# The engines' queue order taken from the tile framework's time-line simulation, in a four-layer encoder kernel

## Chip, cores and metric

The kernel runs on one core of one Trainium2 chip. The metric is the device time of one execution in microseconds: three runs gave 1616.33, 1617.34 and 1620.15, median 1617.34.

## What is computed

The input x is one sequence of 256 tokens with 1024 channels in fp32. Four layers follow one another, each a mixer and an MLP on a residual stream, and a last norm:

```python
for i in range(DEPTH):                       # DEPTH = 4
    kind = i % 3                             # 0: SSD, 1: dilated attention, 2: differential attention
    h = rmsnorm(x, norm_mix_g[i])
    h = ssd_mixer(h, ...) or dilated_mixer(h, ...) or diff_mixer(h, ...)
    x = x + h
    x = x + sqrelu_mlp(rmsnorm(x, norm_mlp_g[i]), mlp_w1[i], mlp_w2[i])
return rmsnorm(x, final_norm_g)
```

So the stages are mix0 (SSD), mlp0, mix1 (dilated), mlp1, mix2 (differential), mlp2, mix3 (SSD), mlp3. The SSD mixer projects h to a gate z, to x, B and C, which pass a convolution of width 5 over time, and to a step width dt; it scans in two directions over chunks of 128 tokens, multiplies with silu(z), norms and projects back. The MLP is square(relu(h @ w1)) @ w2 with 4096 hidden channels.

## The kernel before

Activations lie in SBUF with channels on the partitions and the 256 tokens along the free dimension. All weights are streamed from HBM in chunks of 128 x 1024 fp32. Each chunk goes through three engines: SP issues its load into `raw` (L98, 5 buffers), ACT copies it to the rounded high part `whi` (L110), DVE computes the low part `wlo` = raw - whi (L112; 5 buffers each). PE then does three matmuls for each tile of 128 x 128 (L149 high x high, L150 high x low of the activation, L151 low x high), 256 columns wide. A few chunks of the SSD mixers are used in fp32 as they are (L147).

PSUM banks are named r0 to r3 and a0 to a3. The projections of a mixer alternate between r0 and r1; DVE and ACT empty a bank before its next use. In the SSD mixers a bank of x, B or C is emptied by the convolution: ACT L469, then eight steps of DVE L475 on `cvx`, `cvB` or `cvC`, ACT L477 and DVE L478. A bank of z is emptied by L460 to L463.

At the start of a mixer the norm is finished: PE sums squares over the partitions (`sums`, L274), DVE takes the reciprocal root in small steps (`rsqrt`, L260 to L265) and makes a diagonal matrix `dg` (L282), PE broadcasts it (L283), ACT copies it to `rbc` (L284); then the eight blocks of the normalised activation follow: DVE L304 (`nf`), ACT L305 (high part `nh`), DVE L306 (low part `nl`). The first projections of a mixer (in mix0 and mix3 z0 and z1) use the raw activation (`spl`) instead and are scaled afterwards, so they need no norm.

The step width of an SSD mixer is a chain of some twenty small DVE steps on `dt_t` (`dt_post`, L507 to L529, three of its exponentials on ACT L527). After L521 PE forms running sums with L536 (`dt_sums`), ACT copies them to `rows` (L548) and sends them to DRAM (L550); from there ACT's queue loads them back, broadcast over the partitions, into `bc` (L567, two buffers, 32 loads for both SSD mixers), and DVE adds a mask (L570). ACT's exponentials L595, DVE's product L608 and the scan's matmuls L620 use the result, one pair of `bc` for each of eight groups.

In mix1 the same pattern of projections is followed by scores (L130, L131, L149 to L151 on q and k), the chunks of v (L828 to L830, 384 columns), softmax and output chunks; DVE L142 writes low parts of keys. In mix2 scores, softmax and differences follow.

Two things set the order. The program hands its steps to the framework in an order written by hand: each step has a time in CFG, CFG0, DIL or DIFF, and `emit_events` sorts by it. The framework then builds each engine's queue itself: it runs a simulation of the engines, and puts down an instruction when that simulation finds it ready, the lower number of `tc.cur_priority` first. Only the conversions are shifted in that number, by `TUNE` (L110 and L112, in `_conv`). `take`, `done` and `pump` keep the conversions three to five chunks ahead of their use. An engine works its queue in this order, and an instruction that waits for a semaphore holds back those behind it.

## Time and profile before

| | |
|---|---|
| median of three runs | 1617.34 us |
| the profiled execution's own time | 1616.8 us |
| its span | 1615.0 us |
| PE busy | 1579.2 us, 98% |
| DVE busy | 1193.0 us, 74% |
| ACT busy | 959.2 us, 59% |
| HBM read | 296.41 MB, 186 GB/s over the span |

The stages lie in the span at about: mix0 0 to 257 us, mlp0 to 430, mix1 to 720, mlp1 to 892, mix2 to 1030, mlp2 to 1190, mix3 to 1440, mlp3 to 1590. The profile's page has one row of digits for each engine over 40 equal slices, the busy share in tenths; a row of windows gives busy time and number of instructions for PE, PE's weight load, DVE, ACT and POOL in one stretch, then PE's granted clock as a share of full speed, the DMA share and GB/s. A row of the time line has start, duration, engine, line, operation, output and inputs, and in brackets the idle time of the engine before it with what ended it. A row of waits has the total, how often, and the longest.

### The profile page before, as it was taken

Reading aid. Unit: us, or ns where it says so; the run is one execution under the profiler, and the core shown is the slowest. Engines: PE = TensorE matmul, PEld = TensorE weight load, DVE = VectorE, ACT = ScalarE, POOL = GpSimd, SP = SyncE. Lnnn points to the kernel's source line nnn. Section 1 sums busy time; section 2 is a strip of 40 time slices with the busy share of each in tenths; the row PEclk is TensorE's granted clock in tenths of the full one; section 3 lists DMA queues with packets and bytes.
Section 4 is the critical chain, followed back from the end, with each engine's and each line's share of the span. In section 5 each row is a group of like instructions: output and inputs, shape, how many; then the busy total and the mean of one; then the engine's idle time right before and its main releaser. Section 6 shows DMA issues by size and latency. Waiting matters only on the chain.

```text
span 1615.0 us, 32385 instructions
## 1 busy us (share of the span) xinstructions
PE 1579.2 (98%) x13018; PEld 1534.2 (95%) x13018; DVE 1193.0 (74%) x1996; ACT 959.2 (59%) x1627; POOL 133.1 (8%) x122
## 2 busy tenths in 40 slices
PE   8999999999999999999999999999999999999998
PEld 7989899999989999999999999999998898899997
DVE  6999998555776667666555899755578999985554
ACT  5577866444566666764444677644455777664444
POOL 0012131000200000010000100100010231310001
PEclk9999999999999999999999999999999999999999
DMA  6677765665565555546566575566656677656661
GB/s 210 216 217 235 218 198 177 214 212 188 150 172 166 166 158 168 161 132 200 184 186 190 157 216 151 173 197 191 191 161 183 211 219 226 214 176 190 193 194 65
DMA packets 230294, 299.84 MB, mean 186 GB/s; under 512 B 16496, under 2 KB 166256, under 8 KB 230144
## 3 DMA queue, kind: packets, MB, share of 16 engines
q1 hardware_dynamic: 209552, 262.51, 53.1%
q10 hardware_dynamic: 20592, 35.27, 7.6%
q8 instruction: 102, 1.67, 0.4%
q14 instruction: 48, 0.39, 0.1%
HBM read 296.41 MB, written 3.62 MB: 186 GB/s over the span
## 4 chain that ended last, share of the span: by engine, by line
PE 75%; DVE 13%; DMA 5%; ACT 3%; issue 2%; POOL 0%; SPq 0%; DVEq 0%; ACTq 0%; POOLq 0%
PE r L149 13%; PE r L151 13%; PE r L150 13%; PE a L149 8%; PE a L150 8%; PE a L151 8%; DVE wlo L112 3%; DMA raw<-in_ssd_in_w_dram 2%; PE r L147 2%; DMA bc<-scr 1%; PE a L829 1%; PE a L830 1%; PE a L828 1%; PE r L620 1%; ACT whi L110 1%
## 5 line engine op out<-in xcount | busy, mean ns | idle before, releaser
L112 DVE TENSOR_TENSOR wlo<-raw,whi 128x1024 fp32r<-128x1024 f32 (+1 forms) x490 | 591.3, 1214 | 301.6 <-ACT whi L110 299.9
L110 ACT CAST whi<-raw 128x1024 fp32r<-128x1024 f32 (+1 forms) x490 | 503.1, 1034 | 450.6 <-PE r L150 224.4
L151 PE MATMUL r<-spl,wlo 128*128 128x256 f32 x1248 | 352.1, 282 | 3.7 <-DVE wlo L112 3.7
L149 PE MATMUL r<-spl,whi 128*128 128x256 f32 x1248 | 353.5, 283 | 0.5 <-ACT whi L110 0.5
L150 PE MATMUL r<-spl,whi 128*128 128x256 f32 x1248 | 353.2, 283 | 0.4
L149 PE MATMUL r<-nh,whi 128*128 128x256 f32 (+1 forms) x1024 | 291.6, 285 | 6.7 <-DVE kl L142 3.2
L151 PE MATMUL r<-nh,wlo 128*128 128x256 f32 (+1 forms) x1024 | 286.9, 280 | 2.2 <-DVE wlo L112 2.2
L150 PE MATMUL r<-nl,whi 128*128 128x256 f32 (+1 forms) x1024 | 286.8, 280 | 0.0
L150 PE MATMUL a<-hl,whi 128*128 128x256 f32 x1024 | 286.0, 279 | 0.0
L149 PE MATMUL a<-hh,whi 128*128 128x256 f32 x1024 | 286.0, 279 | 0.0
L151 PE MATMUL a<-hh,wlo 128*128 128x256 f32 x1024 | 285.6, 279 | 0.0
L151 PEld LDWEIGHTS r<-spl,wlo 128*128 128x128 f32 x1248 | 238.5, 191 | 4.3 <-DVE wlo L112 4.1
L150 PEld LDWEIGHTS r<-spl,whi 128*128 128x128 f32 x1248 | 239.1, 192 | 1.3 <-DVE spl L233 1.1
L149 PEld LDWEIGHTS r<-spl,whi 128*128 128x128 f32 x1248 | 238.7, 191 | 1.1 <-ACT whi L110 0.7
L149 PEld LDWEIGHTS r<-nh,whi 128*128 128x128 f32 (+1 forms) x1024 | 193.4, 189 | 11.0 <-issue 6.1
L151 PEld LDWEIGHTS r<-nh,wlo 128*128 128x128 f32 (+1 forms) x1024 | 193.3, 189 | 3.2 <-DVE wlo L112 2.4
L150 PEld LDWEIGHTS r<-nl,whi 128*128 128x128 f32 (+1 forms) x1024 | 193.8, 189 | 0.7 <-DVE nl L306 0.2
L149 PEld LDWEIGHTS a<-hh,whi 128*128 128x128 f32 x1024 | 193.4, 189 | 0.2 <-ACT whi L110 0.2
L150 PEld LDWEIGHTS a<-hl,whi 128*128 128x128 f32 x1024 | 193.5, 189 | 0.0
L151 PEld LDWEIGHTS a<-hh,wlo 128*128 128x128 f32 x1024 | 192.4, 188 | 0.0
L246 POOL TENSOR_TENSOR sqacc<-sqacc,sq 128x256 f32<-128x256 f32 x48 | 43.3, 901 | 1100.8 <-ACT sq L244 1099.1
L595 ACT ACTIVATE e<-bc,tb 128x256 f32<-128x256 f32 (+1 forms) x256 | 95.5, 446 | 1.5 <-issue 1.5
(249 smaller groups left out, 2400.8 us busy)
## 6 DMA issues: line engine op xcount, KB each, us to landing
raw<-in_mlp_w_dram SPq DMA_DIRECT2D x256, 512.0 KB
raw<-in_ssd_in_w_dram SPq DMA_DIRECT2D x96, 512.0 KB
bc<-scr ACTq DMA_DIRECT2D x32, 768.0 KB
raw<-in_dil_qkv_w_dram SPq DMA_DIRECT2D x48, 512.0 KB
raw<-in_ssd_out_w_dram SPq DMA_DIRECT2D x32, 512.0 KB
raw<-in_dil_qkv_w_dram SPq DMA_DIRECT2D x64, 192.0 KB
raw<-in_diff_qkv_w_dram SPq DMA_DIRECT2D x24, 512.0 KB
raw<-in_dil_out_w_dram SPq DMA_DIRECT2D x8, 512.0 KB
```

Source lines behind the costliest of these rows:

```text
L110: self.nc.scalar.copy(out=hi[:, :n], in_=raw[:, :n])
L112: self.nc.vector.tensor_tensor(out=lo[:, :n], in0=raw[:, :n], in1=hi[:, :n].bitcast(F32), op=ALU.subtract)
L147: mm(out, lhsT=wh, rhs=xh, start=start, stop=stop, skip_group_check=True)
L149: mm(out, lhsT=wh, rhs=xh, start=start, stop=False, skip_group_check=True)
L150: mm(out, lhsT=wh, rhs=xl, start=False, stop=False, skip_group_check=True)
L151: mm(out, lhsT=wl, rhs=xh, start=False, stop=stop, skip_group_check=True)
L246: nc.gpsimd.tensor_tensor(out=self.sqs[0], in0=self.sqs[0], in1=sq, op=ALU.add)
L595: X = lambda o, i_, bias: nc.scalar.activation(out=o, in_=i_, func=AF.Exp, bias=bias)
L620: nc.tensor.matmul(b[(h % 2) * 64:(h % 2) * 64 + 64, n * T:(n + 1) * T], lhsT=xt[:, 1 - i, h * 64:(h + 1) * 64], rhs=G[h][:, i * T:(i + 1) ...
L828: mm(o, lhsT=nh[:, k, t], rhs=w_h, start=k == 0, stop=False)
L829: mm(o, lhsT=nh[:, k, t], rhs=w_l, start=False, stop=False)
L830: mm(o, lhsT=nl[:, k, t], rhs=w_h, start=False, stop=k == 7)
```

## The change

`TileContext` gets one more argument. The simulation by which the framework builds the queues is then the one that lays instructions on time lines, instead of the simpler one that it runs by default. The instructions, their shapes and the tiles' names are the same; the order on each engine is another, and with it the wait for each semaphore and the buffer that a tile gets.

```diff
-    with tile.TileContext(nc) as tc:
+    with tile.TileContext(nc, schedule_with_timeline_sim=True) as tc:
         program(tc, aps)
```

The order differs in the mixers and at the beginnings of the stages; the middles of the MLPs have the same order on PE, DVE and ACT before and after, and SP's queue of weight loads is nearly the same. Three places follow. The number behind a name tells tiles of the same name apart.

PE at the start of mix0, before. `r0_275` and `r1_370` are the banks of z0 and z1, `a0_220` that of the norm's sums, `whi_177` and `wlo_178` the high and low part of a chunk of z0's weight:

```order
L149 MATMUL r1_370<-spl_110,whi_206 128x256
L150 MATMUL r1_370<-spl_111,whi_206 128x256
L151 MATMUL r0_275<-spl_150,wlo_178 128x256
L149 MATMUL r0_275<-spl_150,whi_177 128x256
L274 MATMUL a0_220<-guard1024_91,sq0_184 128x1 x4
L150 MATMUL r0_275<-spl_151,whi_177 128x256
```

And after, the end of z0 and z1, with the sums behind them. `r2_337`, `r0_470` and `r1_529` are the banks of dt, x0 and C0:

```order
L150 MATMUL r1_370<-spl_166,whi_212 128x256
L151 MATMUL r1_370<-spl_165,wlo_213 128x256
L274 MATMUL a0_220<-guard1024_91,sq0_184 128x1 x4
L283 MATMUL a0_220<-dg_238,ones_87 128x256
L149 MATMUL r2_337<-nh_243,whi_200 64x256
L149 MATMUL r0_470<-nh_243,whi_302 128x256
L149 MATMUL r1_529<-nh_243,whi_364 128x256
L150 MATMUL r2_337<-nl_244,whi_200 64x256
```

The sums of squares (L274) have moved from between two matmuls of z0 to behind the last of z0 and z1, 65 rows later, and the broadcast (L283) follows them at once.

DVE in mix3, before. `dt_t_14981` is the chain of the step width, `cvx_15129` the convolution of an x unit that leaves bank r1:

```order
L520 SCALAR_TENSOR_TENSOR dt_t_14981<-dt_t_14981 128x128
L475 SCALAR_TENSOR_TENSOR cvx_15129<-r1_15087,vec_76,cvx_15129 128x255
L521 SCALAR_TENSOR_TENSOR dt_t_14981<-dt_t_14981,eal_14807 128x128
L475 SCALAR_TENSOR_TENSOR cvx_15129<-r1_15087,vec_76,cvx_15129 128x255
L524 TENSOR_SCALAR dt_t_14981<-dt_t_14981 128x128
L475 SCALAR_TENSOR_TENSOR cvx_15129<-r1_15087,vec_76,cvx_15129 128x255
L525 TENSOR_SCALAR dt_t_14981<-dt_t_14981 128x128
L475 SCALAR_TENSOR_TENSOR cvx_15129<-r1_15087,vec_76,cvx_15129 128x255
L528 TENSOR_TENSOR dt_t_14981<-dt_t_14981 128x128
L475 SCALAR_TENSOR_TENSOR cvx_15129<-r1_15087,vec_76,cvx_15129 128x254
```

And after, where the same steps of the chain stand in the convolutions of later units (`cvC_15200`, `cvx_15281`):

```order
L520 SCALAR_TENSOR_TENSOR dt_t_14981<-dt_t_14981 128x128
L475 SCALAR_TENSOR_TENSOR cvx_15281<-r1_15239,vec_76,cvx_15281 128x255 x2
L521 SCALAR_TENSOR_TENSOR dt_t_14981<-dt_t_14981,eal_14807 128x128
L475 SCALAR_TENSOR_TENSOR cvx_15281<-r1_15239,vec_76,cvx_15281 128x255
L478 SCALAR_TENSOR_TENSOR cvC_15200<-th_15199,cvC_15200 128x512
L475 SCALAR_TENSOR_TENSOR cvx_15281<-r1_15239,vec_76,cvx_15281 128x255
L524 TENSOR_SCALAR dt_t_14981<-dt_t_14981 128x128
L475 SCALAR_TENSOR_TENSOR cvx_15281<-r1_15239,vec_76,cvx_15281 128x254 x2
L525 TENSOR_SCALAR dt_t_14981<-dt_t_14981 128x128
L475 SCALAR_TENSOR_TENSOR cvx_15281<-r1_15239,vec_76,cvx_15281 128x254 x2
```

From the same conversion (`wlo_15196`) on, L521 has 41 instructions before it now: 5 of L112 (itself among them), 22 of L475, 2 of L478 and 12 steps of the chain. Up to the first L570 they are 65: 6, 33, 4 and 22. Further down the mask on the first rows that come back stands in the middle of the convolution of a B unit (`cvB_15345`):

```order
L475 SCALAR_TENSOR_TENSOR cvB_15345<-r0_15299,vec_76,cvB_15345 128x255 x3
L112 TENSOR_TENSOR wlo_15422<-raw_15278,whi_15421 128x1024
L475 SCALAR_TENSOR_TENSOR cvB_15345<-r0_15299,vec_76,cvB_15345 128x255
L475 SCALAR_TENSOR_TENSOR cvB_15345<-r0_15299,vec_76,cvB_15345 128x254
L570 TENSOR_TENSOR bc_15233<-bc_15233,cst_77 128x4x256
L112 TENSOR_TENSOR wlo_15487<-raw_15308,whi_15486 128x1024
L475 SCALAR_TENSOR_TENSOR cvB_15345<-r0_15299,vec_76,cvB_15345 128x254 x2
L570 TENSOR_TENSOR bc_15236<-bc_15236,cst_77 128x4x256
```

Before, both L570 stood around two steps of `cvx_15281`, with no conversion between them. On PE, L536 stands 34 rows later than before in mix3 (row 9262 instead of 9228) and 22 rows later in mix0 (276 instead of 254).

PE in mix1, before. `r0_5663` and `r1_5740` are the banks of two projections that follow one another:

```order
L151 MATMUL r0_5663<-nh_5183,wlo_5556 128x256
L149 MATMUL r0_5663<-nh_5183,whi_5555 128x256
L150 MATMUL r0_5663<-nl_5184,whi_5555 128x256
L151 MATMUL r0_5663<-nh_5183,wlo_5556 128x256
L149 MATMUL r1_5740<-nh_5183,whi_5590 128x256
L150 MATMUL r1_5740<-nl_5184,whi_5590 128x256
```

And after, where a second set of scores (10 matmuls of L130, L131, L149 to L151 into `r2_5809` and `r3_5810`) and matmuls of v (L828 to L830 into `a0_5842` and `a1_5843`, 17 in all) come between the two; here the last of them:

```order
L828 MATMUL a0_5842<-whi_5720,nh_5183 128x384
L829 MATMUL a0_5842<-wlo_5721,nh_5183 128x384
L830 MATMUL a0_5842<-whi_5720,nl_5184 128x384
L875 MATMUL a2_5835<-head_75,S_5649 128x128 x4
L828 MATMUL a1_5843<-whi_5720,nh_5183 128x384
L829 MATMUL a1_5843<-wlo_5721,nh_5183 128x384
L149 MATMUL r1_5740<-nh_5183,whi_5590 128x256
L150 MATMUL r1_5740<-nl_5184,whi_5590 128x256
```

The first matmul into `r1_5740` has moved behind work that doesn't use that bank. Elsewhere in the mixers the same kind of thing is seen: output chunks of mix0 and mix3 stand up to 20 us earlier on PE, counted in the times that these matmuls had before, and at the starts of mix0 and mix3 DVE has all eight L304 and both L460 ahead of the first L306.

## The prediction

> **What bounds the kernel now.** I read the page first, then the waits of PE, then windows around the longest of them, then time lines of the two places where the order changes most. From the page:
>
> ```profile
> span 1615.0 us, 32385 instructions
> ...
> PE 1579.2 (98%) x13018; PEld 1534.2 (95%) x13018; DVE 1193.0 (74%) x1996; ACT 959.2 (59%) x1627; POOL 133.1 (8%) x122
> ...
> DVE  6999998555776667666555899755578999985554
> ...
> PE 75%; DVE 13%; DMA 5%; ACT 3%; issue 2%; POOL 0%; SPq 0%; DVEq 0%; ACTq 0%; POOLq 0%
> ```
>
> PE is busy for 98% of the span, so all that a new order can take away from PE is the 35.8 us in which it stands (1615.0 - 1579.2), plus the time that it runs at a reduced clock. DVE is at 74% over the whole, but the row of slices has eight or nine tenths in the first six slices and the five around 1240 to 1440 us, which are the two SSD mixers (mix0 and mix3). There DVE has almost nothing to spare, and 13% of the chain goes through it. What PE waits for:
>
> ```profile
> PE r L151 <- DVE wlo L112: 5.8, 2, 3.7
> ...
> PE a L274 <- POOL sqacc L246: 4.5, 3, 2.4
> ...
> PE r L149 <- DVE kl L142: 3.2, 1, 3.2
> ...
> PE r L149 <- DVE cvx L475: 3.2, 4, 1.5
> ...
> PE a L151 <- DVE wlo L112: 2.5, 1, 2.5
> ...
> DVE bc L570 <- DMA bc<-scr: 7.4, 6, 2.5
> ```
>
> Columns: total, times, longest. Few long waits make up most of the 35.8 us: 3.7 for a weight's low part in mix0, 2.4 for a sum of squares at mix1's start, 3.2 for a bank that DVE empties in mix1, 2.5 in mix3's output. The last row is DVE's own: it waits for rows that come back from DRAM.
>
> Windows around the long waits (busy us and number of instructions of each engine, then PE's granted clock):
>
> ```profile
> 14.00:19.00 5.00, 0.85 (x6) 0.45 (x4) 4.79 (x9) 4.71 (x8) 0.00 (x0) 0.98 0.60 214
> ...
> 19.00:26.00 7.00, 6.95 (x33) 6.86 (x34) 5.52 (x13) 0.14 (x1) 0.00 (x0) 0.53 0.70 200
> ...
> 26.00:40.00 14.00, 13.79 (x105) 12.55 (x104) 12.54 (x26) 9.60 (x18) 0.00 (x0) 1.00 0.52 160
> ...
> 436.00:443.00 7.00, 7.00 (x36) 6.95 (x36) 2.82 (x10) 1.26 (x2) 4.41 (x13) 0.57 0.30 79
> ...
> 443.00:475.00 32.00, 31.45 (x248) 31.14 (x248) 26.67 (x48) 21.32 (x38) 0.00 (x0) 1.00 0.68 169
> ...
> 480.00:484.00 4.00, 4.00 (x25) 4.00 (x24) 2.75 (x6) 1.67 (x6) 0.00 (x0) 0.62 0.65 180
> ...
> 1200.00:1204.00 4.00, 4.00 (x23) 4.00 (x23) 2.57 (x9) 1.04 (x1) 0.00 (x0) 0.59 0.29 84
> ```
>
> After each of these waits PE's clock falls to about a half for some microseconds. From 19 to 26 us 33 matmuls take 7.0 us; at the pace of the next row (13.79 / 105 = 0.131 us) they would take 4.3, so 2.7 are lost. From 436: 36 at 31.45 / 248 = 0.127 us make 4.6, so 2.4 lost. From 480: 25 make 3.2, so 0.8 lost; from 1200: 23 make 2.9, so 1.1 lost. [...]
>
> The stages themselves, in equal stretches:
>
> ```profile
> 40.00:80.00 40.00, 39.83 (x288) 37.65 (x287) 38.39 (x83) 21.82 (x47) 2.57 (x2) 1.00 0.69 212
> ...
> 1280.00:1320.00 40.00, 39.82 (x297) 35.43 (x296) 38.93 (x60) 29.21 (x60) 11.97 (x5) 1.00 0.72 225
> ...
> 320.00:360.00 40.00, 40.00 (x342) 40.00 (x342) 22.56 (x22) 18.74 (x21) 0.00 (x0) 1.00 0.70 224
> ...
> 780.00:820.00 40.00, 40.00 (x342) 40.00 (x341) 22.76 (x23) 18.71 (x22) 0.00 (x0) 1.00 0.61 190
> ...
> 1040.00:1080.00 40.00, 40.00 (x355) 40.00 (x354) 23.34 (x23) 19.07 (x23) 0.00 (x0) 1.00 0.64 196
> ...
> 1480.00:1520.00 40.00, 40.00 (x355) 40.00 (x354) 22.46 (x23) 19.21 (x23) 0.00 (x0) 1.00 0.64 195
> ```
>
> In the SSD mixers (the first two) DVE is busy for 38.4 and 38.9 of 40 us and PE for all of it: both bound it, and any wait that falls on DVE is paid again by PE. In the four MLPs PE is full and DVE half empty. There the order of the instructions does not change, but the same matmuls ran at two paces: 342 in 40 us in two of them, 355 in the other two.
>
> **The change part by part.** Nothing is computed differently: PE's 1579 us of work stay. So the sum consists of waits that go, the clock that goes with them, and waits that come. I take the places in order of time.
>
> *Start of mix0.* DVE's low part comes ahead of its copies, so the wait of 3.7 us at 15.1 goes, and the 2.7 us of clock behind it: 6.4 us won. But the norm's sums (L274), which stood on PE in the middle of z0 and z1, now stand behind both. Behind them PE has three matmuls, then the first one that needs the normalised low part nl. That chain, from the rows of before:
>
> ```profile
> 19.65 1.87 PE L274 MATMUL a<-guard,sq 128*128 128x1 f32 x8
> ...
> 21.55 0.16 DVE L260 TENSOR_SCALAR rs_q<-a 128x2 int32<-128x2 int32 x1 [1.36 <-PE a L274]
> ...
> 26.02 0.48 DVE L282 TENSOR_SCALAR dg<-head,rs_y 128x128 f32<-128x128 f32 x2
> ...
> 27.62 0.59 PE L283 MATMUL a<-dg,ones 128*128 128x256 f32 x2
> ...
> 28.25 0.37 ACT L284 COPY rbc<-a 128x256 f32<-128x256 f32 x1 [1.33 <-PE a L283]
> ...
> 28.66 2.07 DVE L304 SCALAR_TENSOR_TENSOR nf<-xT,head,rbc 128x256 f32<-128x256 f32 x5 [0.49 <-ACT rbc L284]
> ...
> 30.64 1.76 DVE L306 TENSOR_TENSOR nl<-nf,nh 128x256 fp32r<-128x256 f32 x5
> ```
>
> z0 and z1 without the stall end at about 25. From L274 to L260 it takes 1.9, six small DVE steps 1.2, L282 0.9, L283 0.6, rbc 0.4, then eight L304 at 0.40 (five took 2.0 from 28.66 to 30.64) 3.2, and now two L460 of 0.6 before the first L306: 25 + 9.4 to 10.1, so nl at about 35. PE has issued some 141 matmuls by then, where before it had issued 163 at 35.1: 22 times 0.131 is 2.9 us behind, with the 6.4 already counted. An idle stretch of nine us then draws the half clock, as the one of 3.7 did: up to 2.7 more. DVE has conversions queued in this time, so I take half of it: 2.9 + 1.4 = **+4.3**, bounds 0 (if DVE runs ahead and makes the lag up) and 5.6.
>
> *The row vectors of mix0.* dt_sums (L536) stands 22 rows later on PE, which is 2.9 us, on top of the lag. The rows come back from DRAM that much later, and L570 waits on DVE in front of the conv steps (L475) that empty PE's banks. Before, the longest such wait, of 2.5 us, fell in this stage, and PE's list has no wait as long on L475. Bounds are 0, as now, and 4.5, the wait that comes out for mix3 below; the lag of the start is partly the same time, so I take **+2**.
>
> *The same chain in mix3*, where the new order is plainest:
>
> ```profile
> 1226.10 1.23 DVE L112 TENSOR_TENSOR wlo<-raw,whi 128x1024 fp32r<-128x1024 f32 x1 [0.16 <-ACT whi L110]
> ...
> 1227.25 0.29 DVE L518 SCALAR_TENSOR_TENSOR dt_t<-dt_t 128x128 f32<-128x128 f32 x1
> ...
> 1229.79 0.28 DVE L521 SCALAR_TENSOR_TENSOR dt_t<-dt_t,eal 128x128 f32<-128x128 f32 x1
> ...
> 1229.99 0.48 DVE L475 SCALAR_TENSOR_TENSOR cvx<-r,vec,cvx 128x255 f32<-128x255 f32 x1
> ...
> 1230.38 0.22 DVE L524 TENSOR_SCALAR dt_t<-dt_t 128x128 f32<-128x128 f32 x1
> ...
> 1231.51 0.41 PE L536 MATMUL r<-cst,dt_t 128*32 128x128 f32 x2
> ...
> 1237.20 0.39 ACTq L567 DMA_DIRECT2D bc<-scr  x1
> ...
> 1243.02 1.23 DVE L570 TENSOR_TENSOR bc<-bc,cst 128x1024 f32<-128x1024 f32 x1 [0.89 <-DMA bc<-scr]
> ...
> 1246.49 1.23 DVE L570 TENSOR_TENSOR bc<-bc,cst 128x1024 f32<-128x1024 f32 x1 [1.45 <-DMA bc<-scr]
> ...
> 1250.11 0.39 PE L149 MATMUL r<-nh,whi 128*128 128x256 f32 x1 [1.51 <-DVE cvx L475]
> ```
>
> Start to start, L112 takes 1.15 us, L475 0.40, a dt step 0.2. Before, L521 begins 3.7 us after the conversion at 1226.10. After, 5 L112, 22 L475, 2 L478 (0.6) and 12 dt steps lie from that conversion up to L521: 5.8 + 8.8 + 1.2 + 2.4 = 18.2, so L521 at 1244.3, 14.5 later. L536, the rows and the load follow it: bc lands at 1257.5 instead of 1243.0, the second at about 1261.0. DVE reaches the first L570 after 6 L112, 33 L475, 4 L478 and 22 dt steps, 6.9 + 13.2 + 2.4 + 4.4 = 26.9, so at 1253.0, and waits 4.5 us there, with five conv steps of cvB and the next conversion behind it; the second L570 adds about 0.4. Before, the two waits together were 0.9 + 1.45, and PE lost 1.5. So DVE loses some 2.6 us more. PE, which needs the bank that cvB holds, then waits up to 5 where it waited 1.5, and the half clock may follow as at 480 (0.8): 3.5 + 0.8 = **+4.3**, bounds 2.6 (DVE's loss alone) and 8.8 (the next pair of rows waits 4.5 as well).
>
> *Start of mix3.* The sums' wait (at most 2.1 of the 4.5) and 1.1 of clock may go, 3.2 in all; but as in mix0 all eight L304 and both L460 now precede the first L306 (3.2 + 1.2, of which PE covers some with the rest of z1), a wait of about 3. By the row of 1200 a wait of this size can draw 1.1 of clock again; I take half: -3.2 + 3 + 0.6 = **+0.4**, bounds -3.2 and +4. [...]
>
> *Inside mix0 and mix3.* Output chunks stand up to 20 us earlier on PE, nearer to their conversions, and fp32 units are broken into more pieces. The waits of 2.2 and 2.5 us on wlo may go or move. DVE's work and so its 38.4 of 40 remain. With the waits that such chunks already have as the price of one (2.2 and 2.5), the bounds are -4.7, both gone, and +9.4, twice as many more; a DVE without slack makes more likely than fewer: **+2.5**, about one more.
>
> *mix1.* At its start the sums come later, so up to 2.4 of wait and 2.4 of clock go, but 48 v matmuls come ahead of the first projection and nl is again spread behind other steps, some 3.5 us of new waits: -1, bounds -4.8 and +1. At 475.9 bank r1 is asked for later: behind a second set of 10 score matmuls and 17 matmuls of v. At 0.117 each for the 256 columns and 0.117 to 0.176 for the 384 these are 3.2 to 4.2 us, as much as the wait of 3.2; it goes, with 0.8 of clock: -4, bounds -4 and 0. Together **-5**.
>
> *mix2 and the MLPs.* mix2 moves by less than 6 us either way and has none of the long waits listed above: **0**, bounds ±3.2, one wait with its clock as at mix3's start. In the MLPs nothing moves, but the pace may come out anew: 40 / 342 - 40 / 355 is 4.3 ns, and some 1415 matmuls at a stretch make 6 us for each MLP. With two of four slow before, the mean is **0**, bounds ±12.
>
> Sum: 4.3 + 2 + 4.3 + 0.4 + 2.5 - 5 + 0 = +8.5 us. The profiled execution took 1616.8 us around its span of 1615.0, which makes 1625.3; the median of the three runs (1617.34) is 0.5 above it, so I forecast **1625.8**.
>
> **The rivals.** *Faster: waits go and what comes is covered.* If DVE overtakes its own queue at the new places, that is, if bc is back before 1253 and nl before 30, then the 6.4 of mix0's start, 4.8 and 4.0 of mix1 and 3.2 of mix3 are won, 18.4 at most; with half of it, 1608. It decides at whether L521 in mix3 begins before about 1240. For it: the rows show these waits plainly, and they are with their clock half as much as all of PE's idle time. Against it: the chain to nl is serial and was covered before by z0 and z1 alone. *No difference: the SSD mixers pay nothing for a later dt,* because bc is double-buffered and DVE makes up the wait with conversions: 8.5 less 4.3, 2 and 2.5 leaves -0.3, 1617. *Much slower: not two but many of the 32 L570 wait.* Loads and masks run one pair behind the other; if each of the sixteen pairs lost 1 us on a DVE without slack, 16 us would come on top, 1640. The 7.4 us in 6 waits of before speak for that only in the first groups.
>
> **How the numbers follow.** Forecast (1618 to 1633) 0.48; faster 0.25; no difference 0.13; much slower 0.14. A measurement here can tell some 0.2%, 3.2 us, from no change. The pace of the MLPs moves each case by 6 either way; so part of the forecast's lower edge counts as no difference and part of the second rival as slower. Faster 0.26, same 0.15, slower 0.59. From 1611, where the faster case lies half inside, to 1641 the range leaves out 2 in 10.
>
> **What would show it.** Right: no wait on wlo before 20 us, PE idle from about 25 to 34 with a clock near 0.5 behind it; L521 of mix3 near 1244 and a wait of over 3 us on bc; no wait on kl near 476. Wrong: nl of mix0 before 31 us; L570 without a wait; or MLP stretches of 40 us that all hold 342, or all 355, with the time of the mixers unchanged.

## The result and the profile after

Four runs of the changed kernel took 1678.59 to 1689.26 us, median 1685.68; four of the kernel before 1613.63 to 1620.15, median 1616.84. The ratio is 1.042 (95%: 1.039 to 1.045): slower by 69 us where 8.5 were forecast. The profiled execution of after took 1684.03 us around a span of 1682.2, which is 67.2 longer than before's. From its page:

```profile
span 1682.2 us, 32474 instructions
...
PE 1597.2 (95%) x13018; PEld 1545.7 (92%) x13018; DVE 1195.5 (71%) x1996; ACT 961.0 (57%) x1627; POOL 121.9 (7%) x122
...
PE   7787889999999999999999999999998989999998
...
DVE  6798698755587666657555898755578998885554
```

PE stands for 85.0 us (1682.2 - 1597.2) instead of 35.8, which is 49.2 of the 67.2; the other 18.0 are matmuls that took longer. DVE has the same work (1195.5 us, before 1193.0) in a longer span, and its share in most of the first slices is down: it waits too. In PE's row the first six slices and those around 1260 to 1400 us have holes: mix0 and mix3. The waits, PE's first:

```profile
PE r L149 <- DVE cvx L475: 10.8, 2, 7.9
PE r L587 <- ACT cb L579: 6.4, 1, 6.4
PE r L149 <- DVE cvB L475: 6.0, 3, 2.8
PE r L149 <- DVE z L460: 5.2, 2, 2.7
...
PE r L151 <- DVE wlo L112: 1.2, 2, 0.8
...
PE a L274 <- POOL sqacc L246: 0.4, 1, 0.4
```

```profile
DVE bc L570 <- DMA bc<-scr: 21.0, 13, 5.3
...
DVE bc L570 <- ACT cvC L469: 7.2, 1, 7.2
```

The waits that the prediction wanted gone are gone: L151's on `wlo`, z0's of 3.7 us among them, from 5.8 to 1.2 us, `sqacc` from 4.5 to 0.4, and `kl` is not in the list any more. In their place PE waits for banks that a convolution empties (L475), and DVE waits for the rows of the step width 14 times, 28.2 us, where it waited 6 times, 7.4 us. Windows of after (columns as before):

```profile
26.00:36.00 10.00, 2.94 (x9) 1.60 (x9) 8.07 (x24) 5.08 (x13) 0.00 (x0) 0.67 0.52 158
36.00:44.00 8.00, 8.00 (x55) 7.97 (x55) 4.21 (x10) 1.76 (x4) 0.00 (x0) 0.78 0.01 2
...
80.00:120.00 40.00, 30.99 (x203) 27.61 (x204) 36.59 (x50) 31.04 (x72) 9.79 (x7) 0.83 0.66 199
...
360.00:400.00 40.00, 40.00 (x342) 40.00 (x341) 22.37 (x22) 19.13 (x23) 0.00 (x0) 1.00 0.63 191
820.00:860.00 40.00, 40.00 (x355) 40.00 (x355) 23.26 (x23) 19.16 (x23) 0.00 (x0) 1.00 0.64 197
...
1540.00:1580.00 40.00, 40.00 (x342) 40.00 (x341) 20.26 (x19) 17.35 (x19) 0.00 (x0) 1.00 0.63 185
```

and the stretch of mix0 that compares with the third, before:

```profile
80.00:120.00 40.00, 40.00 (x300) 35.33 (x299) 38.86 (x63) 31.44 (x65) 6.47 (x5) 1.00 0.74 226
```

203 matmuls instead of 300 in 40 us, at a granted clock of 0.83: here is the loss, far behind the start of the stage, where the first two rows stand. By stage, counted from one norm's broadcast (L283) to the next, the lengths before and after are:

| | mix0 | mlp0 | mix1 | mlp1 | mix2 | mlp2 | mix3 | mlp3 |
|---|---|---|---|---|---|---|---|---|
| before, us | 261.6 | 180.6 | 291.0 | 177.2 | 122.4 | 171.5 | 238.1 | 172.5 |
| after, us | 310.6 | 179.0 | 290.2 | 169.7 | 126.6 | 169.3 | 263.4 | 173.5 |
| difference | +49.0 | -1.6 | -0.9 | -7.6 | +4.2 | -2.3 | +25.3 | +1.1 |

By these borders the two SSD mixers cost 74.3 us, and all else gives 7.1 back. But the broadcast itself stands at another place among PE's matmuls after, so the borders move by several us. PE's lag, that is by how much the changed kernel starts its n-th matmul later than before's n-th, is free of that in the middles of the MLPs, where the order is the same, and good to an us or two near them. It is 46.1 us at 262 us of before's time, 45.5 at 430, 43.4 at 730, 38.4 at 890, 40.6 at 1040, 41.3 at 1195, 61.2 at 1440 and 67.3 at the end. So mix0 costs 46.1 and mix3 19.9; mix1 gives 2.1 and mlp1 5.0; mix2 costs 2.2 and mlp3 6.1. Inside the SSD mixers the lag grows like this: in mix0 it is -6 us at 30 us of before's time, +4 at 40, +19 at 80, +25 at 110 and +47 at 170; in mix3 it falls from 41.3 at 1195 us to 37.6 at 1204 and is 41.9 at 1224, 50.2 at 1264 and 59.1 at 1324.

How such a loss arises shows in the time line of after around PE's longest wait. One unit of x (`cvx`) must leave its bank by eight steps of L475:

```profile
193.03 0.37 ACTq L567 DMA_DIRECT2D bc<-scr  x1
...
200.94 1.23 DVE L570 TENSOR_TENSOR bc<-bc,cst 128x1024 f32<-128x1024 f32 x1 [7.21 <-ACT cvC L469]
202.08 1.22 DVE L112 TENSOR_TENSOR wlo<-raw,whi 128x1024 fp32r<-128x1024 f32 x1
203.22 0.87 DVE L475 SCALAR_TENSOR_TENSOR cvx<-r,vec,cvx 128x255 f32<-128x255 f32 x2
204.00 1.22 DVE L112 TENSOR_TENSOR wlo<-raw,whi 128x1024 fp32r<-128x1024 f32 x1
205.13 0.87 DVE L475 SCALAR_TENSOR_TENSOR cvx<-r,vec,cvx 128x255 f32<-128x255 f32 x2
...
207.05 1.22 DVE L570 TENSOR_TENSOR bc<-bc,cst 128x1024 f32<-128x1024 f32 x1
...
208.97 0.86 DVE L475 SCALAR_TENSOR_TENSOR cvx<-r,vec,cvx 128x254 f32<-128x254 f32 x2
209.75 1.22 DVE L608 TENSOR_TENSOR G<-e,cb 128x1024 f32<-128x1024 f32 x1
...
214.72 0.87 DVE L475 SCALAR_TENSOR_TENSOR cvx<-r,vec,cvx 128x254 f32<-128x254 f32 x2
...
215.64 0.58 PE L149 MATMUL r<-nh,whi 128*128 128x256 f32 x1 [7.93 <-DVE cvx L475]
```

DVE first stands for 7.2 us at a mask: its rows were asked for at 193.03 only. (The profile names ACT's L469, which ended at 200.9. But the mask reads only `bc` and a constant, and in the trace the last of the updates of the loads' semaphore that the mask waits for comes at 200.85 us, 7.8 us after the load was issued.) Behind the mask in the queue stand the eight steps. They take 12.4 us, 203.22 to 215.59, because conversions, another mask, products and steps of another unit stand between them. PE waits for the bank and loses 7.9 us, and its clock with it: the granted clock is 0.60 from 207.7 to 220.5 us.

### The profile page after: what moved, and what is told of

It reads as the page before. It is cut to its first block, busy times and chain, and to the rows that moved or that the text cites. A ratio compares the mean times of both kernels' runs of the same rounds, so it can differ in the third digit from the quotient of the medians.

```text
span 1682.2 us, 32474 instructions
## 1 busy us (share of the span) xinstructions
PE 1597.2 (95%) x13018; PEld 1545.7 (92%) x13018; DVE 1195.5 (71%) x1996; ACT 961.0 (57%) x1627; POOL 121.9 (7%) x122
## 5 line engine op out<-in xcount | busy, mean ns | idle before, releaser
L112 DVE TENSOR_TENSOR wlo<-raw,whi 128x1024 fp32r<-128x1024 f32 (+1 forms) x490 | 593.4, 1214 | 349.1 <-ACT whi L110 340.4
L110 ACT CAST whi<-raw 128x1024 fp32r<-128x1024 f32 (+1 forms) x490 | 504.9, 1034 | 515.8 <-PE r L150 281.2
L149 PE MATMUL r<-spl,whi 128*128 128x256 f32 x1248 | 346.4, 280 | 6.0 <-ACT spl L746 3.9
L150 PE MATMUL r<-spl,whi 128*128 128x256 f32 x1248 | 348.4, 280 | 0.8 <-DVE spl L233 0.8
L151 PE MATMUL r<-spl,wlo 128*128 128x256 f32 x1248 | 346.6, 279 | 1.2 <-DVE wlo L112 1.2
L149 PE MATMUL r<-nh,whi 128*128 128x256 f32 (+1 forms) x1024 | 298.3, 292 | 29.2 <-DVE cvx L475 10.8
L150 PE MATMUL r<-nl,whi 128*128 128x256 f32 (+1 forms) x1024 | 291.7, 285 | 0.0
L151 PE MATMUL r<-nh,wlo 128*128 128x256 f32 (+1 forms) x1024 | 291.0, 284 | 0.0
L151 PE MATMUL a<-hh,wlo 128*128 128x256 f32 x1024 | 284.7, 279 | 0.0
L149 PE MATMUL a<-hh,whi 128*128 128x256 f32 x1024 | 283.4, 279 | 0.3 <-ACT hh L353 0.3
L149 PEld LDWEIGHTS r<-spl,whi 128*128 128x128 f32 x1248 | 234.0, 189 | 8.2 <-ACT spl L746 4.7
L150 PEld LDWEIGHTS r<-spl,whi 128*128 128x128 f32 x1248 | 235.1, 189 | 2.1 <-DVE spl L233 1.2
L151 PEld LDWEIGHTS r<-spl,wlo 128*128 128x128 f32 x1248 | 234.5, 188 | 1.6 <-DVE wlo L112 1.5
L149 PEld LDWEIGHTS r<-nh,whi 128*128 128x128 f32 (+1 forms) x1024 | 198.8, 194 | 37.4 <-issue 13.4
L150 PEld LDWEIGHTS r<-nl,whi 128*128 128x128 f32 (+1 forms) x1024 | 198.6, 194 | 0.8 <-issue 0.4
L151 PEld LDWEIGHTS r<-nh,wlo 128*128 128x128 f32 (+1 forms) x1024 | 198.2, 194 | 0.1
L149 PEld LDWEIGHTS a<-hh,whi 128*128 128x128 f32 x1024 | 192.3, 189 | 0.7 <-ACT hh L353 0.5
L151 PEld LDWEIGHTS a<-hh,wlo 128*128 128x128 f32 x1024 | 192.2, 188 | 0.0
L595 ACT ACTIVATE e<-bc,tb 128x256 f32<-128x256 f32 (+1 forms) x256 | 92.6, 445 | 24.7 <-DVE bc L570 10.7
```

The costliest lines, as they stand in the source:

```text
L110: self.nc.scalar.copy(out=hi[:, :n], in_=raw[:, :n])
L112: self.nc.vector.tensor_tensor(out=lo[:, :n], in0=raw[:, :n], in1=hi[:, :n].bitcast(F32), op=ALU.subtract)
L149: mm(out, lhsT=wh, rhs=xh, start=start, stop=False, skip_group_check=True)
L150: mm(out, lhsT=wh, rhs=xl, start=False, stop=False, skip_group_check=True)
L151: mm(out, lhsT=wl, rhs=xh, start=False, stop=stop, skip_group_check=True)
L595: X = lambda o, i_, bias: nc.scalar.activation(out=o, in_=i_, func=AF.Exp, bias=bias)
```

## The experiments

The first theory was the prediction's third rival: masks (L570) that wait for late rows stall DVE. Against it stood that one queue, DVE's or PE's or ACT's, is put into a bad order in some other way, and that something besides the order (buffers, semaphores, the queue of SP) costs the time. All kernels below but `start_and_mix1` have the option on. Dependences without a semaphore then hold chosen instructions of an engine in a chosen order; the rest is left to the new simulation. For a whole queue (shortened):

```diff
-        program(tc, aps)
+        program(tc, aps), pin(tc)
+ORDER = {"DVE": "..."}                      # numbers of the instructions, in the order of before
+def pin(tc):
+    by = {i.name: i for i in tc.nc.cur_bb.bb.instructions}
+    for t in ORDER.values():
+        seq = [by["I-%d" % n] for n in unpack(t)]
+        for p, q in zip(seq, seq[1:]):
+            tc.add_manual_dep(q, p.name, NoSync, reason="order")
```

and for single instructions, q behind p (shortened):

```diff
+AFTER = {693: 737, 696: 743, 837: 813, ...}
+    for q, p in AFTER.items():
+        tc.add_manual_dep(by["I-%d" % q], "I-%d" % p, NoSync, reason="order")
```

Each ratio is to the kernel before, run in turn with it on the same chip (its medians there were 1606 to 1610 us).

**One queue as before, two new.** `ORDER` has one engine.

> The new simulation orders every engine except DVE, whose whole queue is held in the order of before. Theory A (the loss sits in DVE's queue: masks L570 that wait for bc with convolution steps behind them, and dt steps that come late): most of the 68 us comes back, 1616 to 1635. Theory B (the loss sits in PE's queue: output chunks placed up to 100 matmuls earlier chase their conversions): 1660 to 1685. Theory C (the loss sits in ACT's queue: conversions L110 behind exponentials L595 that wait): 1660 to 1685.

> The new simulation orders every engine except PE, whose queue is held in the order of before. Theory A (DVE's queue): 1660 to 1690, mask waits on bc still over 20 us in all. Theory B (PE's queue): 1616 to 1640. Theory C (ACT's queue): 1660 to 1690.

> The new simulation orders every engine except ACT, whose queue is held in the order of before. Theory A (DVE's queue): 1650 to 1690, since the masks and the dt steps still stand where the new order puts them, though bc is asked for at the old place in ACT's queue. Theory B (PE's queue): 1660 to 1690. Theory C (ACT's queue): 1616 to 1640.

Measured: DVE as before 1.044 (1.041 to 1.046), PE as before 1.078 (1.075 to 1.082), ACT as before 1.050 (1.046 to 1.054). Putting any one queue back does not help, and PE's makes it far worse. With DVE's own old queue the masks wait 6.2 us, less than before, and the time is still that of after: the waits on `bc` can't be the whole.

**The 32 masks behind the instruction that they followed before.** `AFTER` has 32 pairs, all of L570.

> The new order, with 32 constraints: each mask L570 has to stand on DVE behind the instruction that stood directly ahead of it before. Theory A in its narrow form (early masks alone): DVE's waits on bc fall from 28 us to under 12, and the time by about as much, to 1655 to 1668. Theories B and C: 1678 to 1690, no change beyond noise.

Measured 1.039 (1.035 to 1.042). The waits on `bc` fall from 28.2 us to these:

```profile
DVE bc L570 <- DMA bc<-scr: 8.4, 9, 3.7
```

The profiled execution, the fastest of the four with 1656.2 us where the median is 1669.7, has by the borders of the table mix0 at +33.8 instead of +49.0 us, and the median gains next to nothing. So with nearly all of these waits gone most of the loss stays.

**All three queues as before, and two of three.** `ORDER` has PE, DVE and ACT, or two of them.

> The option of the change, with the queues of PE, DVE and ACT all three held in the order of before; GpSimd's and SyncE's are still the new ones. Theory D (the loss lies in the orders as a set: the three queues have to fit each other, whichever of them the new simulation makes): within 8 us of the kernel before, 1605 to 1620. Theory E (something else that the option changes, such as buffers, semaphore waits, or the load queue): 1650 or more.

> PE's and DVE's queues as before, ACT's from the new simulation. Theory D: a queue that doesn't fit the two others costs 15 to 45 us, 1625 to 1655. Theory C (ACT's queue carries the loss after all): 1655 to 1690. If ACT is harmless: 1605 to 1620.

> PE's and ACT's queues as before, DVE's from the new simulation. Theory D: 1625 to 1665, and DVE, which has the least to spare in the SSD mixers, should cost the most of the three. Theory A (DVE's queue alone): 1655 to 1690, with over 15 us of DVE's waits on bc.

> DVE's and ACT's queues as before, PE's from the new simulation. Theory D: 1620 to 1650, from output chunks that PE reaches before their conversions. Theory B (PE's queue alone): 1655 to 1690.

| new queues | ratio (95%) |
|---|---|
| none of the three | 1.003 (1.001 to 1.006) |
| PE | 1.016 (1.012 to 1.020) |
| ACT | 1.031 (1.024 to 1.038) |
| DVE | 1.053 (1.048 to 1.058) |
| PE and ACT | 1.044 (1.041 to 1.046) |
| PE and DVE | 1.050 (1.046 to 1.054) |
| DVE and ACT | 1.078 (1.075 to 1.082) |
| all (after) | 1.042 (1.039 to 1.045) |

The first row settles that the option costs by the order of these three queues: the option is on, SP's and POOL's queues are left as it makes them, and 0.3% remains. Each queue alone costs, 1.6 + 3.1 + 5.3 = 10.0% in all, more than the 4.2% of the three together: the new queues partly fit one another, and none is the culprit. DVE's alone costs most, and the same unit of `cvC` in mix0 shows one way in which it can. Before, on DVE's time line:

```profile
123.07 3.20 DVE L475 SCALAR_TENSOR_TENSOR cvC<-r,vec,cvC 128x255 f32<-128x255 f32 x8
```

With DVE's queue alone new:

```profile
136.31 0.87 DVE L475 SCALAR_TENSOR_TENSOR cvC<-r,vec,cvC 128x255 f32<-128x255 f32 x2
137.09 1.22 DVE L112 TENSOR_TENSOR wlo<-raw,whi 128x1024 fp32r<-128x1024 f32 x1
138.22 1.65 DVE L475 SCALAR_TENSOR_TENSOR cvC<-r,vec,cvC 128x255 f32<-128x255 f32 x4
139.79 1.21 DVE L112 TENSOR_TENSOR wlo<-raw,whi 128x1024 fp32r<-128x1024 f32 x1
140.92 0.47 DVE L475 SCALAR_TENSOR_TENSOR cvC<-r,vec,cvC 128x254 f32<-128x254 f32 x1
141.31 1.21 DVE L608 TENSOR_TENSOR G<-e,cb 128x1024 f32<-128x1024 f32 x1
142.44 0.47 DVE L475 SCALAR_TENSOR_TENSOR cvC<-r,vec,cvC 128x254 f32<-128x254 f32 x1
```

Two conversions and a product have moved in among the eight steps, and the bank comes free after 6.6 us instead of 3.2. PE's waits in this run:

```profile
PE r L149 <- DVE cvB L475: 12.9, 4, 5.3
PE r L149 <- DVE cvx L475: 12.2, 4, 5.9
```

Over the 32 units (first L475's start to the last one's end) the median is 3.20 us before, 6.46 after and 5.71 here. Two theories followed from it. One (G): the new simulation puts preparations, that is conversions, masks, products on DVE and casts and exponentials on ACT, where they look ready, ahead of the steps that free PE's banks, and this is the loss. The other (I): the spread of the eight steps itself is.

**DVE's queue alone new, preparations held behind the instruction that they followed before.** `ORDER` has PE and ACT; `AFTER` all 490 conversions L112, the 64 masks and products L570 and L608, or all 554.

> PE and ACT as before, DVE from the new simulation as in the run that took 1.053 times the time of before, but each conversion L112 has to stand on DVE behind the instruction that stood directly ahead of it before. Theory G (DVE's queue costs because work that prepares something, conversions L112, masks L570 and products L608, stands ahead of the convolution steps that free PE's banks): ratio 1.015 to 1.035, the conversions being the most numerous. Theory H (no kind of instruction is at fault, any queue that doesn't fit the others costs this much): 1.045 to 1.06.

> The same with the masks L570 and the products L608 held and the conversions free. Theory G: ratio 1.025 to 1.04, and DVE's waits on bc fall from 24 us to under 12. Theory H: 1.045 to 1.06.

> The same with all three kinds held (L112, L570, L608). Theory G: ratio 1.00 to 1.015. Theory H: 1.035 or more, since 1165 of the rows of DVE's queue still differ from those of before.

Measured against 1.053: 1.031 (1.026 to 1.036), 1.038 (1.034 to 1.041), and all 1.013 (1.010 to 1.017), three quarters of the loss gone; the units' median is 3.71 us, and what PE waits for on `cvB` is down from 12.9 us:

```profile
PE r L149 <- DVE cvB L475: 2.3, 2, 1.5
```

**ACT's queue alone new, its casts L110 and exponentials L595 held so.**

> PE and DVE as before, ACT from the new simulation as in the run that took 1.031, with ACT's conversions L110 and exponentials L595 held behind what stood ahead of them before. Theory G also for ACT: ratio under 1.012. Theory H: 1.025 or more.

Measured 1.011 (1.008 to 1.015), where the free queue had 1.031. So for DVE's queue alone and for ACT's alone, most of the cost goes when the preparations are held. Whether holding as many other instructions would do the same was not tried.

**The whole new order with the preparations of both held.** No `ORDER`; `AFTER` for L112, L570, L608, L110 and L595.

> The whole new order, no queue held, but the preparing instructions have to stand behind what stood directly ahead of them before: L112, L570 and L608 on DVE, L110 and L595 on ACT. Theory G: ratio 1.01 to 1.025 (PE's own queue cost 1.016 when it alone was new). Theory H: 1.035 to 1.06.

Measured 1.036 (1.033 to 1.039): G fails for the three queues together. In this trace mix0 is 22 us behind by 80 us, with a wait that is new at this length, that of DVE's first step of the step width (8.5 us of it in mix0, 5.0 in mix3):

```profile
DVE dt_t L507 <- PE r L502: 13.5, 2, 8.5
```

DVE reaches L507 before PE's matmuls for it are done and stands, with the steps that free the banks behind it in its queue. From 80 to 170 us the lag grows by 4 us only, where in after it grew by 28.

**The starts of the two SSD mixers as before** (all three engines up to 75 us and from 1193 to 1262 us), the rest new, and **both together**.

> The whole new order, except that at the starts of mix0 and mix3 (what ran before 75 us, and between 1193 and 1262 us) PE, DVE and ACT keep the order of before. If the starts and the interiors each carry a part (theory G with its starts): ratio 1.02 to 1.033. If the starts carry nearly all, as my prediction had it: under 1.012. If they carry nothing: 1.04 or more.

> Both: starts as before, and in the rest the preparing instructions (L112, L570, L608 on DVE, L110, L595 on ACT) held behind what stood ahead of them before; all else, PE's queue from 75 us on among it, is the new order. Theory G with its starts: ratio 0.997 to 1.015. Theory H (any queue that doesn't fit the others): 1.025 or more.

Measured 1.038 (1.033 to 1.042), between the forecasts for a part and for nothing, and 1.020 (1.017 to 1.023). With the starts held the lag of mix0 at 80 us is 2 us instead of 19, and at 180 it is 36 all the same; meanwhile the waits on the masks, 28.2 us in after, have grown:

```profile
DVE bc L570 <- DMA bc<-scr: 36.1, 17, 7.8
```

Both together remove half of the loss, neither does it alone, and 2.0% stays: by the lag, counted as above, mix0 +7, mix1 +2, mix2 +8 and mix3 +4 us. More was expected to go (1.015 at most). Which queue holds this rest was not isolated.

**The convolution steps themselves.** In the first kernel `ORDER` is after's, with the eight L475 of each of the 32 units in a row at the place of the first; in the second it is before's, with 45 L112 moved in between the steps of the unit ahead of them.

> The new order on every engine, except that on DVE the eight convolution steps L475 of each of the 32 units stand in a row, at the place of the first of them. Theory I (what costs is that other instructions stand between the steps that empty a bank, so that PE gets it back 3 us later): ratio 1.01 to 1.027 instead of 1.042. Theory J (the steps lie in the shadow of other waits, such as those on bc; the interleaving is a symptom): 1.035 or more.

> The option with the queues of PE, DVE and ACT in the order of before (1.003 times before), except that 45 conversions L112 that stood behind a convolution unit on DVE now stand between its steps, up to three for each unit; each takes 1.15 us. Theory I: up to 45 x 1.15 = 52 us of later banks, of which PE feels a third to two thirds: ratio 1.013 to 1.025. Theory J: 1.00 to 1.008.

Measured: together in the new order 1.048 (1.044 to 1.052), no gain; spread in the old order 1.036 (1.032 to 1.040). In the second the units' median is 6.18 us, close to after's, and PE's waits have after's kind:

```profile
PE r L149 <- DVE cvx L475: 20.4, 9, 5.0
```

By the ratios this kernel lost 3.2 points against all queues as before, 52 us of 1610. That 45 conversions of 1.15 us make 52 us too is chance: the 32 units together hold their banks for 206.8 us, where with all queues as before it is 124.7, so 82 us more. Some 51 of these are conversions, 46 now inside a unit instead of 2. Another 31 are time in which DVE stands inside a unit at such a conversion, because ACT has not yet made its high part; in after, DVE stands so for 0.6 us inside the units. PE felt 52 of the 82, where a third to two thirds of the conversions' 52 alone had been expected. How much of the loss is the work and how much these waits was not separated. In the first kernel the median is 3.20 us again, and other waits have taken over, on DVE and on PE:

```profile
DVE bc L570 <- DMA bc<-scr: 38.6, 15, 7.4
```

```profile
PE r L587 <- DVE cvx L478: 8.4, 1, 8.4
PE a L151 <- DVE wlo L112: 7.8, 3, 3.6
```

So spreading conversions through the units, with the waits for ACT that it brings, costs 3.2 points in the old order, where the whole change costs 4.2; but undoing the spread in the new order gives nothing back. I is shown to be able to cost this much, not to be what costs it in the new order.

**The parts of the change that looked good, in the old order.** Without the option; `ORDER` is before's with mix1 in the new order, and z0's `wlo` ahead of the copies and the last four L274 behind z0.

> The kernel before with two pieces of the new order and no option: mix1's instructions in the new order among themselves, and in mix0 the first late conversion L112 ahead of the sums of squares, with the norm's four L274 behind z0. If these pieces are worth what the traces show there (5 us in mix1, 2 to 6 at the start): ratio 0.992 to 0.996. If the pieces only fit the queues around them in the new order: 0.998 to 1.01.

Measured 0.999 (0.996 to 1.002) in 12 runs, which can't be told from no change. In the trace the start is not shorter. By the borders of the table mix1 is 3.7 us shorter, but by the count of matmuls PE is 5.3 us ahead of before at 430 us, from a faster mlp0, and 5.4 ahead at 730: mix1 won nothing. No version beat the kernel before.

## Why the prediction was wrong

The direction and the starts were right, the size was an eighth. Point by point.

*Start of mix0: right.* From the time line of after:

```profile
25.31 1.05 PE L274 MATMUL a<-guard,sq 128*128 128x1 f32 x8 [0.32 <-DVE sq L201]
...
29.40 1.22 PE L283 MATMUL a<-dg,ones 128*128 128x256 f32 x2 [3.04 <-DVE dg L282]
...
35.08 1.15 PE L149 MATMUL r<-nh,whi 128*128 128x256 f32 x2 [2.56 <-DVE z L460]
35.44 1.09 DVE L306 TENSOR_TENSOR nl<-nf,nh 128x256 fp32r<-128x256 f32 x3
```

L274 stands at 25.3 (25 predicted), `nl` at 35.4 (about 35); PE idles in between and its clock is 0.67 and then 0.78 in the windows above. The lag at 40 us is 3.9 (+4.3).

*The row vectors of mix0: mechanism right, far too small.* The lag grows from 3.9 to 18.7 between 40 and 80 us of before's time, 15 where +2 was taken and 4.5 was the upper bound. Of these, 5 come up to 60 us, ahead of the first mask, with a wait of 2.8 us for a bank of `cvx`. The other 10 come around the first mask, which alone waits 5.3 us, until 80.0; PE stands for 6.4 us at L587 in the same place, and its clock is 0.83 from 80 to 120 us. The bound was mix3's wait carried over, with none of PE's banks and none of the clock behind it counted.

*mix3: the start right, the chain inside its bounds for another reason.* The start was to win 3.2 and lose 3.6 (+0.4). The lag falls by 3.7 between 1195 and 1204 us, where before had the sums' wait of 1.9 us and a clock of 0.59 behind it, and rises by 4.3 up to 1224: +0.6. As predicted, a wait of 2.7 us for L460 stands there, and clock went with it:

```profile
1245.00:1255.00 10.00, 7.23 (x44) 6.58 (x44) 8.96 (x19) 5.44 (x12) 0.00 (x0) 0.83 0.43 117
```

PE stood for 2.8 us in these ten and the clock was 0.83; before, at mix1's start, a wait of 2.4 us was followed by 0.57 from 436 to 443 us. Then DVE's two rows:

```profile
1286.34 0.28 DVE L521 SCALAR_TENSOR_TENSOR dt_t<-dt_t,eal 128x128 f32<-128x128 f32 x1
...
1300.14 1.23 DVE L570 TENSOR_TENSOR bc<-bc,cst 128x1024 f32<-128x1024 f32 x1 [0.60 <-DMA bc<-scr]
```

The span is some 41 us behind at mix3's start (1245.3 against 1204.4), so L521 comes about 15 us later in the stage, as the 14.5 had it. But the mask waits 0.6 us and not 4.5: DVE itself was late, having waited for ACT (2.3 us in front of `cvB`) and worked through the queue. The lag still grew by 8 from 1224 to 1264 us of before's time (+4.3, bounds 2.6 and 8.8).

*Inside mix0 and mix3: the step that failed.* Here stood +2.5, bounds -4.7 and +9.4, "about one more" wait of the size that `wlo` already had. Measured are 46.1 - 18.7 = 27 us in mix0 and 61.2 - 50.2 = 11 in mix3. The step priced the new order by the long waits of the old one. It saw that "units are broken into more pieces" and took it for a matter of output chunks; it never asked what the pieces do to the time for which a bank is held, though the price of that stood in a row: 1.15 us for each preparation inside a unit, on an engine that is busy for 38.4 of 40 us. That conversions inside the units can cost 52 us, with the waits that they bring, is shown by `before_conv_spread`; that they are what cost the 38 us here is not shown, since `after_conv_together` gained nothing. What the runs do show in place of the step is that the order of the three queues as a whole costs this, and no single kind of wait. The third rival named a part of it, many masks that wait (14 of 32 did), with 16 us and a chance of 0.14; holding the masks showed that they are a part and not the cause.

*mix1: the waits went, and most of the gain went again.* The waits on `sqacc` and the 3.2 us of `kl` are gone. By the lag PE won 1.8 us between 430 and 475 us of before's time (-1 predicted), though a new wait stands behind the later norm:

```profile
PE a L828 <- ACT nh L305: 1.6, 1, 1.6
```

It won 5.2 more up to 500 us (-4 predicted). But from there to 730 us it lost 4.9 again, with no wait of PE over 0.4 us and a granted clock of 1.00: the matmuls follow one another a little more slowly (on average 121.0 ns from start to start instead of 118.5), and why is open. Over the stage this makes -2.1 where -5 was predicted.

*mix2 and the MLPs.* By the lag mix2 costs 2.2 us, inside 0 ±3.2; its largest new wait, at its end, is for ACT:

```profile
PE r L149 <- ACT spl L746: 3.9, 4, 1.6
```

The MLPs moved inside ±12 and nearly cancel: mlp1 ran at 355 matmuls in 40 us instead of 342 and won 5.0, mlp3 at 342 instead of 355 and lost 6.1. Two of the four are slow in both traces.

One reading ahead of the sum was off as well: the four long waits named there add up to 11.8 of PE's 35.8 us, a third and not most.

Shown is that the order of the three queues is the cause, that conversions put inside the bank-freeing steps, with the waits that they bring, cost 3.2 points in the old order, and that holding the masks or the starts takes 15 and 17 us out of their own stretch of mix0 and is worth only 0.3 and 0.5 points at the end. A single seat of the loss was not found: with each cure alone in the whole new order other waits stood in the place of the ones removed. Open is the last 2.0% with preparations and starts held, 8 us of which lie in mix2.

## What to carry to other kernels

When a scheduler rewrites the queues, measure for each buffer that the bound engine needs how long it is held, first to last step, and price what has moved into that stretch by its duration and by what it waits for there; on this DVE, busy for 38.4 of 40 us in mix0 before, 52 of 82 us held longer were lost. Don't price a new order by the waits of the old one: those are what an order that fits has left over. And don't cure such an order one wait at a time or one queue at a time; here the queues of engines that hand buffers to one another had to fit together.

## What the runs showed of the hardware

The same fp32 matmuls in the MLPs ran at one of two paces, 342 or 355 in 40 us at a granted clock of 1.00. With the same order it was 342 in mlp1 before and 355 after, and 355 in mlp3 before and 342 after; in `start_and_mix1` it was 356 and 355 in mlp0 and mlp1, where before had 342:

```profile
320.00:360.00 40.00, 40.00 (x356) 40.00 (x355) 23.56 (x23) 18.68 (x21) 0.00 (x0) 1.00 0.74 231
...
780.00:820.00 40.00, 40.00 (x355) 40.00 (x354) 22.59 (x23) 19.79 (x23) 0.00 (x0) 1.00 0.61 193
```

From start to start that is 117.8 or 113.3 ns, and it moved an MLP by 5 to 6 us. Whether the pace also changes between executions of one kernel no trace shows, so that it is why runs of the kernel before lie between 1600.72 and 1622.92 us on one chip is only argued. Eight steps of L475 in a row take 3.20 us though one takes 0.47: on DVE they start 0.39 us apart. They alternate between the two halves of the unit, so that each works on the result of the step two ahead of it.
